# A decoder layer with four mixers on one core: one product with ones in place of four in the Conformer norm, and other places and loads for the MLP's forms and last weights

## The chip, the core and the metric

The kernel runs on one core of one Trainium2 chip. The core has five engines, which work side by side and each take their instructions in order: TensorE (PE) multiplies matrices into PSUM, VectorE (DVE), ScalarE (ACT) and GpSimd (POOL) work elementwise, and SyncE (SP) issues DMA transfers. POOL and ACT issue transfers too. PE appears in two rows of the profile: PE for the products, PEld for the weight loads, which run beside them. SBUF is the memory that the engines work in, DRAM the large one behind it.

The metric is device microseconds (us) of one launch, as the median of the runs. Besides, one execution was taken by the hardware profiler; every row of the trace comes from that one.

## The reference, cut to what matters

One layer of a decoder is computed for 1024 prompt tokens and 8 x 8 sample tokens, 1088 in all, with D = 1024 and everything in float32:

```python
h = rmsnorm(x, norm_mix_g) * (1 + sc1) + sh1
# four mixers, each 512 wide, from one input projection of h:
# HGRN2, RWKV-7, Conformer convolution, RG-LRU
u = cf[..., :W] * sigmoid(cf[..., W:])
yc = causal_dwconv(s_cf, u, cf_dw, cf_dw_b)
mu = mean(yc); var = mean(square(yc - mu))           # over the 512 channels
y_cf = silu((yc - mu) * rsqrt(var + 1e-5) * cf_ln_g + cf_ln_b)
out = sum_b(sigmoid(h @ w_gate + b_gate)_b * (y_b @ w_branch_b)) @ w_out
x = x + g1 * out
h2 = rmsnorm(x, norm_mlp_g) * (1 + sc2) + sh2
x = x + g2 * (square(relu(h2 @ w_mlp1)) @ w_mlp2)    # 1024 -> 4096 -> 1024
y = rmsnorm(x, norm_final_g)
```

The states of the mixers are outputs as well. The scales, shifts and factors sc, sh and g come from a small projection of a conditioning vector, one for the prompt and one for each of the eight samples.

## The kernel before, in words

**Layout.** Channels lie on the partitions and tokens along the free axis, so a tile is 128 channels by up to 1088 tokens. The tokens are cut in three ways: in CHUNKS of 364, 362 and 362, in two halves (columns) of 544, and in four quarters of 272 (QU).

**Products.** A float32 product is made of three products in the faster fp32r type: both factors are split into a rounded high part and the low rest, and hi x hi, lo x hi and hi x lo are added up in PSUM. `split` (L308) does it: ACT writes the high part, DVE subtracts it for the low part. `weights` (L151) does this for a block of four 128 x 128 weights: SP loads it into `wst` (3 buffers), and the split goes to `whi` and `wlo` (4 buffers). Products with `ones`, a 128 x 128 matrix of ones, sum over the partitions; they are in plain float32, which the trace records as two passes for each.

**The order of the work.** The program is laid out when it is built: a scheduler with a model of each engine's time decides the order of the instructions on every engine, by their dependencies and by priorities (`high_priority(offset=PRIO)` draws weights and evacuations ahead). Tiles of one tag rotate through a fixed number of buffers, and a pool that is closed gives its space to the pools opened after it. So where a tile lies decides what it must wait for.

**Stages.** 1. The first norm. 2. The mixers: the string ROUNDS lists, in four rounds, the steps of RWKV (r), HGRN2 (h), the Conformer (c), the RG-LRU (l), the Conformer norm (n, in the last round only), the conditioning (a) and the 32 gate products (g), which depend on nothing but h and fill PE while the recurrences run. 3. The merge of the branches, in the order RG-LRU, RWKV, Conformer, HGRN2. 4. The output projection with `w_out`, one half of the tokens after the other; POOL's queue writes the new x to DRAM (`xsp`). 5. MLP1. 6. MLP2 with the last norm.

**The Conformer norm**, `cf_norm` (L971). The four channel tiles X[0] to X[3] of 128 channels come back from DRAM. For each of the three chunks, four products with ones (L980-981) add the tiles up into `cm`, DVE subtracts the mean from each (L983), ACT squares each and four more products with ones (L988) give `cvar`. Ln and Exp make the inverse root, and the scaled tiles go back to DRAM for the merge.

**MLP1** (L1340-1388) uses seven products of blocks where a 2 x 2 block product has eight (Strassen's scheme in Winograd's form). `column_forms(c)` (L1284) normalises the half c of x and makes the seven forms B11, B21, T1 to T4 and B22 of it, each of them four tiles of 272 columns, split in high and low. The pools `resb` and `resa` hold x's two halves on the right of SBUF; the forms and `xw` (further weight forms) stand on the left, in the place of the output projection's pools. `seven_weights` (L212) loads four blocks of W1, makes seven forms of them and splits each; the first four forms made go to the pool `wp`, the others to `xw`. `seven` (L263) issues the seven products of one of 16 pairs of hidden blocks, and `evac` squares the positive part, splits it and writes it to DRAM (`asc`) by POOL's queue. Column 1's forms are made after the output projection, with twice the usual priority, and the first weights are asked for after them.

**MLP2** (L1391-1463) sums over 32 hidden blocks in six GROUPS. The first two blocks are kept in SBUF (`KK`). The others are loaded by SP's queue into tiles `ah` and `al` of 1088 columns, NA = 9 buffers of each; a block's high and its low tile have 544 KB each. `gemm_quarters` (L186) makes the products of one group for one of eight output tiles, and `ev` adds the result to R[mt]; in the second group (gi = 1) the saved x is loaded as `xr`, in one buffer, and added as well. The last group goes through the tokens in three columns of work: quarters (0, 1), quarter 2, quarter 3, each over eight output tiles, and builds its weights anew for each. Behind each column stands its norm (L1448-1462): one product with ones for each quarter, Ln, Exp, and the scaling of eight tiles, by ACT and POOL for columns 1 and 2 and for tiles 2 and 5 of column 3, else by DVE.

Of the kernel before, what the change touches and what calls it, by code (L numbers as in the profile page):

```python
# [31 lines left out]
GN_EPS = 64e-5  # L32
LN_EPS = 1e-5
# [57 lines left out]
class Net:  # L91
# [59 lines left out]
    def weights(self, ap, prio=True):  # L151

        with self.tc.high_priority(offset=PRIO) if prio else nullcontext():
            st = self.wp.tile([128, 4, 128], F32, name="wst", tag="wst", bufs=WST)
            hi = self.wp.tile([128, 4, 128], F32R, name="whi", tag="whi", bufs=WHI)
            lo = self.wp.tile([128, 4, 128], F32R, name="wlo", tag="wlo", bufs=WHI)
# [29 lines left out]
    def gemm_quarters(self, parts, X, evac, groups):  # L186
# [4 lines left out]
        for j, (ap, ks) in enumerate(parts):  # L191
            hi, lo = self.weights(ap)
# [57 lines left out]
    def product(self, ps, W, X, cs, start=True):  # L250

        hi, lo = W
        xh, xl = X
        for c in cs:
            for i in range(4):
                self.mm(ps[:, c, :QU], hi[:, i, :], xh[c][i], start=start and i == 0, stop=False)
                self.mm(ps[:, c, :QU], lo[:, i, :], xh[c][i], start=False, stop=False)
                self.mm(ps[:, c, :QU], hi[:, i, :], xl[c][i], start=False, stop=i == 3)
# [712 lines left out]
    def cf_norm(self):  # L971
# [121 lines left out]
PRIO = 3000  # L1093
WST, WHI = 3, 4
# [7 lines left out]
def trunk_kernel(ctx: ExitStack, tc: tile.TileContext, A):  # L1102
# [147 lines left out]
    pools = right(last, "resb"), right(ractx, "resa")  # L1250
# [18 lines left out]
    def add_sq(acc, r, mt, pool):  # L1269
        t = pool.tile([128, HALF], F32, name="sqt", tag="sqt", bufs=2)[:, :r.shape[-1]] if mt else None  # L1270
        net.sumsq(acc, r, t)
# [12 lines left out]
    def column_forms(c):  # L1284
# [9 lines left out]
        def split_form(f, i, src):  # L1294
            net.split(F[f][0][c][i], F[f][1][c][i], src)

# [7 lines left out]
        part = lambda k, h: R[:, k, h * QU:h * QU + QU]  # L1304
        for f, o in (("B11", 0), ("B21", 4)):
            for i in range(4):
                normed(i + o)
                split_form(f, i, part(i + o, 0))

        for f, out, a, b in (("T1", (0, 0), (0, 1), (0, 0)), ("T2", (0, 0), (4, 1), (0, 0)),  # L1310
                             ("T3", (0, 1), (4, 1), (0, 1)), ("T4", (4, 0), (4, 0), (0, 0))):
            for i in range(4):
                net.tt(part(i + out[0], out[1]), part(i + a[0], a[1]), part(i + b[0], b[1]), OP.subtract)
                split_form(f, i, part(i + out[0], out[1]))
        for i in range(4):
            split_form("B22", i, part(i + 4, 1))

    with ExitStack() as m:
# [8 lines left out]
        for half in range(2):  # L1327
            R, accs, rstd = RR[half]
            for mt in range(8):
                def ev(ps, n0, n):  # L1330
                    r = R[:, mt, n0:n0 + n]
                    add_resid(r, half * HALF + n0, ps[:, :n], n, mt, 2)
                    add_sq(accs[:, n0:n0 + n], r, mt, ops[half])
# [7 lines left out]
    for c in range(2):  # L1341
        fpool = left(fctx, f"forms{c}")
        for f in F:
            for p in range(2):
                F[f][p][c] = [fpool.tile([128, QU], F32R, name=f"{f}{'hl'[p]}{c}{i}") for i in range(4)]
    net.xw = left(fctx, "xw")
    column_forms(0)
    net.stage.close()
    with tc.tile_pool(name="pq", bufs=4, space=PSUM, reuse_waits="tile") as net.pq:
# [8 lines left out]
        with ExitStack() as m:  # L1358
# [17 lines left out]
            for j in range(16):  # L1376
                W = net.seven_weights((A["w1"][2 * j], A["w1"][2 * j + 1]))
# [10 lines left out]
        fctx.close()  # L1388


        with ExitStack() as m:  # L1391
            rp, ap_ = left(m, "resid"), left(m, "ap")
# [3 lines left out]
            GROUPS = ((0, 1), (2, 3, 4, 5, 6, 7), tuple(range(8, 16)), tuple(range(16, 24)), (24, 25, 26, 27), (28, 29, 30, 31))  # L1396
# [16 lines left out]
            for gi, ks in enumerate(GROUPS):  # L1413
                final = gi == len(GROUPS) - 1
                Xs = {}
                for k in ks:
                    if gi == 0:
                        Xs[k] = Kept(2 * k), Kept(4 + 2 * k)
                    else:
                        t = [ap_.tile([128, NT], F32R, name=f"a{p}", tag=f"a{p}", bufs=NA) for p in "hl"]  # L1420
                        for x, d in zip(t, asc):
                            nc.sync.dma_start(x.bitcast(F32), d[k].bitcast(F32))
# [3 lines left out]
                def ev(ps, qs):  # L1426
# [6 lines left out]
                    if final:  # L1433
                        sl = slice(qs[0] * QU, qs[-1] * QU + QU)
                        add_sq(accs[:, sl], r[:, sl], mt, ap_)

                for cs in (((0, 1),), ((2,),), ((3,),)) if final else (((0, 1), (2, 3)),):
                    for mt in range(8):
# [117 lines left out]
```

## Time and profile before

| | us |
|---|---|
| runs (3) | 2477.72, 2475.24, 2478.2 |
| their median | 2477.72 |
| the profiled execution | 2474.55 |
| its span, first to last instruction | 2472.8 |
| DVE, ACT and POOL busy | 1375.8, 1035.5, 306.0 |

The profile's span is 1.75 us shorter than the same execution's time. Busy times are those of instructions that compute; issuing a transfer, waiting and branching are not counted. A row of a timeline names the line of the code and the operation, then output<-input by the names of the tiles, the shape of the input or output, and xN, where N instructions of one kind are taken together. Where a helper records an operation, all its uses have the helper's line (L98 for ACT, L101 and L104 for DVE, L107 for PE), and the names of the tiles tell them apart. The granted clock is the share of full speed that PE was allowed.

### The profile page before, as it was taken

What the parts mean: (1) busy time and instruction counts of PE and PEld (TensorE: products, weight loads), DVE (VectorE), ACT (ScalarE), POOL (GpSimd) and SP (SyncE); (2) the same over time, 40 slices, a digit from 0 to 9 for tenths busy, and PEclk for the clock granted to TensorE, in tenths of its full rate; (3) what the DMA queues carried; (4) which work ended last, traced back from release to release, by engine and by line L of the source; (5) the groups of instructions that cost most, each with busy time, mean ns of one, the idle gap of its engine ahead of it and who ended that gap; (6) DMA issues with size and microseconds to landing.
All of it is one profiled execution on the core that took longest, in us unless ns stands there. A gap on an engine that the chain in (4) does not pass through costs nothing.

```text
span 2472.8 us, 46690 instructions
## 1 busy us (share of the span) xinstructions
PE 2394.4 (97%) x19150; PEld 2236.7 (90%) x19150; DVE 1375.8 (56%) x2540; ACT 1035.5 (42%) x1849; POOL 306.0 (12%) x479
## 2 busy tenths in 40 slices
PE   6999999999999999999999999997999999999996
PEld 4998898988998988889888999997999998999996
DVE  6666445746266473656734676768655552422247
ACT  5522545225344234542256553455666663111115
POOL 0102200012101021000111000001222221000003
PEclk9999999999999999999999999999999999999998
DMA  7333221241322232213322464532655657425244
GB/s 258 129 88 95 94 70 63 80 111 57 106 69 70 81 94 91 74 64 85 100 90 107 148 215 164 175 120 89 184 155 154 158 151 266 156 100 189 68 153 135
DMA packets 189140, 300.45 MB, mean 122 GB/s; under 512 B 57320, under 2 KB 105400, under 8 KB 188928
## 3 DMA queue, kind: packets, MB, share of 16 engines
q1 hardware_dynamic: 138512, 217.79, 27.9%
q0 software_dynamic: 47104, 74.44, 9.9%
q10 hardware_dynamic: 3312, 5.25, 0.6%
q8 instruction: 150, 2.46, 0.4%
q14 instruction: 62, 0.51, 0.1%
HBM read 211.29 MB, written 81.66 MB: 118 GB/s over the span
## 4 chain that ended last, share of the span: by engine, by line
PE 83%; DVE 7%; DMA 4%; ACT 3%; issue 2%; SPq 0%; ACTq 0%; DVEq 0%; POOL 0%; POOLq 0%
PE pg L107 57%; PE pa L107 6%; PE pe L107 4%; PE sm L107 2%; PE pc L107 2%; PE pb L107 2%; PE pu L107 2%; DVE X L101 2%; PE ada L107 1%; PE G L107 1%; PE pyr L107 1%; PE po L107 1%; DMA adaw<-ada 1%; DVE wlo L101 1%; DMA g<-gst 1%
## 5 line engine op out<-in xcount | busy, mean ns | idle before, releaser
L107 PE MATMUL pg<-Hh,whi 128*128 128x362 f32 (+1 forms) x1872 | 625.9, 335 | 1.0 <-ACT gst L98 0.7
L107 PE MATMUL pg<-Hh,wlo 128*128 128x362 f32 (+1 forms) x1872 | 626.6, 335 | 0.0
L107 PE MATMUL pg<-Hl,whi 128*128 128x362 f32 (+1 forms) x1872 | 621.0, 334 | 0.0
L98 ACT ACTIVATE whi<-wst 128x512 fp32r<-128x512 f32 (+1 forms) x404 | 250.0, 620 | 609.7 <-PE pg L107 534.8
L101 DVE TENSOR_TENSOR wlo<-wst,whi 128x512 fp32r<-128x512 f32 (+1 forms) x404 | 278.5, 690 | 380.9 <-ACT whi L98 380.1
L107 PEld LDWEIGHTS pg<-Hh,whi 128*128 128x128 f32 x1872 | 352.6, 188 | 12.5 <-issue 2.3
L107 PEld LDWEIGHTS pg<-Hl,whi 128*128 128x128 f32 x1872 | 352.3, 189 | 8.5 <-DVE Hl L104 0.8
L107 PEld LDWEIGHTS pg<-Hh,wlo 128*128 128x128 f32 x1872 | 352.9, 189 | 7.6
L107 PE MATMUL pg<-ah,whi 128*128 128x272 f32 x960 | 276.4, 290 | 2.9 <-ACT whi L98 2.9
L107 PE MATMUL pg<-ah,wlo 128*128 128x272 f32 x960 | 277.3, 290 | 1.4 <-DVE wlo L101 1.4
L107 PE MATMUL pg<-al,whi 128*128 128x272 f32 x960 | 273.8, 290 | 0.0
L107 PEld LDWEIGHTS pg<-ah,whi 128*128 128x128 f32 x960 | 181.9, 190 | 3.5 <-ACT whi L98 3.3
L107 PEld LDWEIGHTS pg<-ah,wlo 128*128 128x128 f32 x960 | 182.1, 190 | 2.2 <-DVE wlo L101 2.0
L107 PEld LDWEIGHTS pg<-al,whi 128*128 128x128 f32 x960 | 180.3, 190 | 0.0
L104 DVE SCALAR_TENSOR_TENSOR cacc<-u,pv,cacc 128x1024 f32<-128x1024 f32 x120 | 153.8, 1281 | 2.1
L104 DVE SCALAR_TENSOR_TENSOR R<-pg,mod,R 128x544 f32<-128x544 f32 (+2 forms) x120 | 65.7, 570 | 136.7 <-PE pg L107 136.7
L107 PE MATMUL pg<-yh,whi 128*128 128x362 f32 (+1 forms) x384 | 127.5, 332 | 1.1 <-DVE gt L101 1.1
L107 PE MATMUL pg<-yh,wlo 128*128 128x362 f32 (+1 forms) x384 | 126.6, 330 | 0.0
L107 PE MATMUL pg<-yl,whi 128*128 128x362 f32 (+1 forms) x384 | 126.2, 329 | 0.0
L1181 POOL DMA_DIRECT2D g<-gst x96 | 53.5, 557 | 390.0 <-ACT gst L98 377.5
L98 ACT ACTIVATE gst<-pg 128x362 f32<-128x362 f32 (+1 forms) x96 | 45.4, 473 | 126.2 <-PE pg L107 111.6
L699 POOL TENSOR_SCALAR sp<-St,dec 128x64 f32<-128x64 f32 x60 | 58.5, 975 | 229.2 <-DVE St L104 208.0
(443 smaller groups left out, 4757.3 us busy)
## 6 DMA issues: line engine op xcount, KB each, us to landing
wst<-w SPq DMA_DIRECT2D x136, 256.0 KB, 3.3
adaw<-ada SPq DMA_DIRECT2D x48, 512.0 KB, 7.2
wst<-w_in SPq DMA_DIRECT2D x92, 256.0 KB, 2.9
gt<-g SPq DMA_DIRECT2D x32, 544.0 KB, 4.1
wst<-w_gate SPq DMA_DIRECT2D x64, 256.0 KB, 2.9
ah<-ah POOLq DMA_DIRECT2D x60, 272.0 KB, 2.7
al<-al POOLq DMA_DIRECT2D x60, 272.0 KB, 4.3
ah<-ah SPq DMA_DIRECT2D x30, 544.0 KB, 9.0
```

Source lines behind the costliest of these rows:

```text
L98: return self.nc.scalar.activation(out, in_, func, bias=bias, scale=scale)
L101: return self.nc.vector.tensor_tensor(out, a, b, op=op)
L104: return self.nc.vector.scalar_tensor_tensor(out, a, s, b, op0=op0, op1=op1)
L107: return self.nc.tensor.matmul(out, lhsT, rhs, start=start, stop=stop, skip_group_check=True)
L699: nc.gpsimd.tensor_scalar(sp, St, dec[:, c:c + 1], None, op0=OP.mult)
L1181: nc.gpsimd.dma_start(d[:, n0:n0 + n], t[:, :n])
```

## The change

**The Conformer norm.** The four tiles of a chunk are added on DVE into `acc`, a slice of the tile that the inverse root uses later, and one product with ones is made of it. The squares are summed into the same slice by `sumsq` (L395: ACT squares, DVE adds), and again one product is made.

```diff
+            acc = rs_[:, n0:n0 + n]
+            self.tt(acc, X[0][:, n0:n0 + n], X[1][:, n0:n0 + n], OP.add)
+            for j in (2, 3):
+                self.tt(acc, acc, X[j][:, n0:n0 + n], OP.add)
             ps = self.pgt("cm")
-            for j in range(4):
-                self.mm(ps[:, :n], self.ones, X[j][:, n0:n0 + n], start=j == 0, stop=j == 3)
+            self.mm(ps[:, :n], self.ones, acc)
...
+            for j in range(4):
+                self.sumsq(acc, X[j][:, n0:n0 + n], self.lp.tile([128, 364], F32, name="gst", bufs=2)[:, :n] if j else None)
             ps = self.pgt("cvar")
-            for j in range(4):
-                s = self.lp.tile([128, 364], F32, name="gst", bufs=2)[:, :n]
-                self.act(s, X[j][:, n0:n0 + n], AF.Square)
-                self.mm(ps[:, :n], self.ones, s, start=j == 0, stop=j == 3)
+            self.mm(ps[:, :n], self.ones, acc)
```

**The weight forms' place and the column forms.** `xw` moves to the right side, between the pools of x's two halves. Which of the seven weight forms lie in `wp` and which in `xw` changes. The first pair's weights, W0, are asked for after column 0's forms, before column 1's. The four tiles of a form become one tile of four slices (and `product` picks a slice); column 0's steps take four slices at once, column 1's two.

```diff
-                pool = self.wp if next(n) < 4 else self.xw
+                pool = self.wp if next(n) in (0, 1, 5, 6) else self.xw
...
-    pools = right(last, "resb"), right(ractx, "resa")
+    xctx = ExitStack()
+    pools = [right(last, "resb")]
+    net.xw = right(xctx, "xw")
+    pools.append(right(ractx, "resa"))
...
+        step = 2 if c else 4
+        part = lambda k, h: R[:, k:k + step, h * QU:h * QU + QU]
+
+        def split_form(f, i, src):
+            net.split(F[f][0][c][:, i:i + step], F[f][1][c][:, i:i + step], src)
...
-                F[f][p][c] = [fpool.tile([128, QU], F32R, name=f"{f}{'hl'[p]}{c}{i}") for i in range(4)]
-    net.xw = left(fctx, "xw")
+                F[f][p][c] = fpool.tile([128, 4, QU], F32R, name=f"{f}{'hl'[p]}{c}")
     column_forms(0)
+    W0 = net.seven_weights((A["w1"][0], A["w1"][1]))
     net.stage.close()
...
-                W = net.seven_weights((A["w1"][2 * j], A["w1"][2 * j + 1]))
+                W = net.seven_weights((A["w1"][2 * j], A["w1"][2 * j + 1])) if j else W0
```

**MLP2's loads.** The first loaded group has two blocks in place of six, the big groups follow, and POOL's queue issues the loads. The pools are opened in another order, so that the `ah` and `al` tiles come to lie lowest, and `xr` and the last norm's squares move to a pool of their own.

```diff
-            rp, ap_ = left(m, "resid"), left(m, "ap")
+            ap_, rp, mp = left(m, "ap"), left(m, "resid"), left(m, "misc")
...
-            GROUPS = ((0, 1), (2, 3, 4, 5, 6, 7), tuple(range(8, 16)), tuple(range(16, 24)), (24, 25, 26, 27), (28, 29, 30, 31))
+            GROUPS = ((0, 1), (2, 3)) + tuple(tuple(range(i, i + 8)) for i in (4, 12, 20)) + ((28, 29, 30, 31),)
...
-                            nc.sync.dma_start(x.bitcast(F32), d[k].bitcast(F32))
+                            nc.gpsimd.dma_start(x.bitcast(F32), d[k].bitcast(F32))
```

**The last group's weights and norm.** The eight blocks of the last group's weights are built once, in the first column, into a pool `fw` with eight buffers, which takes the place of `resb`, and are used again in the other columns. The norm of a column becomes a function `last_norm`, issued after the third output tile of the next column. DVE does the scaling in one instruction, except for tiles 2 and 5 of column 3.

```diff
+                if final:
+                    last.close()
+                    fw, kept = right(m, "fw"), []
+                for n, qs in enumerate(columns):
+                    for mt in range(8):
...
+                            if n == 0:
+                                kept.append(net.weights(A["w2"][ks[0] // 4, mt], pool=fw, bufs=8))
+                            net.gemm_quarters([(kept[mt], ks)], Y, ev, (qs,))
...
+                        if final and n and mt == 2:
+                            last_norm(columns[n - 1])
+                if final:
+                    last_norm(columns[-1])
...
                     for k in range(KB8):
                         r, t = R[k][:, sl], rstd[:, sl]
-                        if cs[0] != (3,) or k % 3 == 2:
+                        if qs == (3,) and k % 3 == 2:
                             net.act(r, r, AF.Copy, scale=net.p("norm_final_g", k))
                             nc.gpsimd.tensor_tensor(r, r, t, op=OP.mult)
                         else:
                             net.stt(r, r, net.p("norm_final_g", k), t, OP.mult, OP.mult)
```

More of the change, by code (lines that the diff above doesn't have):

```diff
@@ L32 @@
 GN_EPS = 64e-5
+PRIO = 3000
+WST, WHI = 3, 4
 LN_EPS = 1e-5
@@ L148, in pgt, with weights @@
         return self.pg.tile([128, 512], F32, name=name, tag="pg")
-    def weights(self, ap, prio=True):
+    def weights(self, ap, prio=True, pool=None, bufs=WHI):
         with self.tc.high_priority(offset=PRIO) if prio else nullcontext():
             st = self.wp.tile([128, 4, 128], F32, name="wst", tag="wst", bufs=WST)
-            hi = self.wp.tile([128, 4, 128], F32R, name="whi", tag="whi", bufs=WHI)
-            lo = self.wp.tile([128, 4, 128], F32R, name="wlo", tag="wlo", bufs=WHI)
+            hi = (pool or self.wp).tile([128, 4, 128], F32R, name="whi", tag="whi", bufs=bufs)
+            lo = (pool or self.wp).tile([128, 4, 128], F32R, name="wlo", tag="wlo", bufs=bufs)
             n = ap.shape[1]
@@ L190, in gemm_quarters @@
         xh, xl = X
-        for j, (ap, ks) in enumerate(parts):
-            hi, lo = self.weights(ap)
+        for j, (W, ks) in enumerate(parts):
+            hi, lo = W if isinstance(W, tuple) else self.weights(W)
             for g, qs in enumerate(groups):
@@ L1090, in lru_block @@
         nc.gpsimd.dma_start(self.ysc[3][j], hs[:, :NT])
-PRIO = 3000
-WST, WHI = 3, 4
 NG = 5
@@ L1267, in add_resid, with add_sq @@
                 net.tt(r[:, e:n], r[:, e:n], t.rearrange("p s t -> p (s t)"), OP.add)
-    def add_sq(acc, r, mt, pool):
-        t = pool.tile([128, HALF], F32, name="sqt", tag="sqt", bufs=2)[:, :r.shape[-1]] if mt else None
+    def add_sq(acc, r, mt, pool, width):
+        t = pool.tile([128, width], F32, name="sqt", tag="sqt", bufs=2)[:, :r.shape[-1]] if mt else None
         net.sumsq(acc, r, t)
@@ L1434, in ev, with last_norm @@
                         sl = slice(qs[0] * QU, qs[-1] * QU + QU)
[L1435 to L1454 removed]
+                        add_sq(accs[:, sl], r[:, sl], mt, mp, HALF)
+                def last_norm(qs):
+                    sl = slice(qs[0] * QU, qs[-1] * QU + QU)
+                    ps = net.pqt("rms")
+                    for i, q in enumerate(qs):
+                        s = slice(q * QU, q * QU + QU)
+                        net.mm(ps[:, i, :QU], net.ones, accs[:, s])
+                        net.lnp(rstd[:, s], ps[:, i, :QU], 1.0 / D, net.eps)
+                        net.exph(rstd[:, s])
                     for k in range(KB8):
                         r, t = R[k][:, sl], rstd[:, sl]
[L1457 removed]
+                        if qs == (3,) and k % 3 == 2:
                             net.act(r, r, AF.Copy, scale=net.p("norm_final_g", k))
@@ L1462, in trunk_kernel @@
                         (nc.sync if k % 2 else nc.scalar).dma_start(A["y"][k][:, sl], r)
-    last.close()
+                columns = ((0, 1), (2,), (3,)) if final else (((0, 1), (2, 3)),)
+                if final:
[3 more added lines that the diff above has]
+                    for mt in range(8):
+                        if not final:
+                            net.gemm_quarters(parts(ks, mt), Y, ev, qs)
+                        else:
+                            if n == 0:
+                                kept.append(net.weights(A["w2"][ks[0] // 4, mt], pool=fw, bufs=8))
+                            net.gemm_quarters([(kept[mt], ks)], Y, ev, (qs,))
+                        if gi == 1:
+                            x = mp.tile([128, NT], F32, name="xr", tag="xr", bufs=1)
+                            for h in range(2):
+                                nc.sync.dma_start(x[:, h * HALF:h * HALF + HALF], xsp[h][:, mt, :])
+                            net.tt(R[mt], R[mt], x, OP.add)
+                        if final and n and mt == 2:
+                            last_norm(columns[n - 1])
+                if final:
+                    last_norm(columns[-1])
 def _pack(i):
```

35 lines of the change are left out of this document (10 added, 25 removed).

## The prediction

> **What bounds the kernel now.** I read the page first, then PE's waits, then a table of busy time by stage, and only then single rows. The page's head, and PE's busy tenths in 40 slices of 61.8 us:
>
> ```profile
> span 2472.8 us, 46690 instructions
> ...
> PE 2394.4 (97%) x19150; PEld 2236.7 (90%) x19150; DVE 1375.8 (56%) x2540; ACT 1035.5 (42%) x1849; POOL 306.0 (12%) x479
> ...
> PE   6999999999999999999999999997999999999996
> ```
>
> TensorE (PE) is busy for 97% of the span. Only three of its slices fall below 9: the first, which the change does not touch, the one near 1700 us, and the last. So time is to be had in two ways: take products away where PE never rests, or fill those holes. The longest entries of PE's waits that the change can touch (total us, times, longest):
>
> ```profile
> PE rms L107 <- DVE accs L101: 13.0, 3, 8.2
> ...
> PE pe L107 <- DVE x L101: 2.8, 1, 2.8
> PE pe L107 <- ACT whi L98: 2.5, 1, 2.5
> PE pe L107 <- DVE wlo L101: 2.5, 1, 2.5
> ```
>
> Busy time by stage, from the windows view: window, its length, then busy us (and instructions) of PE, weight loads, DVE, ACT, POOL, then the granted clock, DMA share and GB/s:
>
> ```profile
> 1296.00:1330.00 34.00, 33.51 (x213) 24.12 (x214) 8.94 (x20) 14.96 (x30) 3.33 (x7) 1.00 0.07 25
> 1350.00:1386.00 36.00, 34.63 (x615) 32.81 (x614) 35.41 (x54) 25.92 (x34) 2.85 (x5) 1.00 0.44 149
> 1690.00:1740.00 50.00, 37.18 (x238) 34.02 (x237) 43.08 (x97) 34.21 (x84) 7.97 (x15) 0.90 0.33 93
> 1699.00:1733.00 34.00, 22.45 (x127) 20.28 (x128) 33.74 (x78) 25.07 (x65) 3.58 (x7) 0.85 0.24 66
> 1750.00:2050.00 300.00, 300.00 (x2383) 300.00 (x2382) 171.38 (x262) 179.42 (x308) 76.75 (x112) 1.00 0.59 155
> 2060.00:2100.00 40.00, 34.37 (x252) 33.12 (x251) 9.73 (x24) 13.30 (x29) 1.35 (x2) 0.96 0.93 330
> 2100.00:2420.00 320.00, 320.00 (x2551) 320.00 (x2550) 112.31 (x232) 44.93 (x71) 0.00 (x0) 1.00 0.38 133
> 2420.00:2462.00 42.00, 31.19 (x223) 30.17 (x221) 33.28 (x60) 24.20 (x48) 19.66 (x16) 0.88 0.49 153
> ```
>
> The two long MLP rows give PE's pace when nothing holds it: 300/2383 = 0.126 us a product of 272 columns. Against that pace I count what each disturbed window loses, idle time and slowed clock together. MLP1's start: 238 x 0.126 = 30.0 us of 50, so 20 lost. MLP1 to MLP2: 252 x 0.126 = 31.8 of 40, so 8 lost. The last window: 223 x 0.126 = 28.1 of 42, of which I give 1 back for the slower f32 products of the norm, so 13 lost. The four parts of the change sit on these three windows and on the Conformer norm.
>
> **Part A, the Conformer norm.** PE's timeline there (start, length, instruction; a product in f32 counts as two passes):
>
> ```profile
> 1297.12 2.61 PE L107 MATMUL cm<-cx,ones 128*128 128x364 f32 x8
> 1299.65 0.34 PE L107 MATMUL pst<-vk 128*64 128x64 f32 x4
> ...
> 1307.52 1.49 PE L107 MATMUL cvar<-gst,ones 128*128 128x364 f32 x4
> 1308.94 0.44 PE L107 MATMUL pu<-p,G 64*64 64x64 f32 x4
> ```
>
> Eight passes take 1299.65 - 1297.12 = 2.53 us, 0.63 a product; four of the variance 1.42, 0.71 a product. Each chunk keeps one of four, so nine of each go: 9 x 0.63 + 9 x 0.71 = 12.1 us of PE. PE was busy 33.51 of those 34 us, and what fills it (the gate products) is left, so all of it could count. In exchange DVE gets three adds of tiles and three of squares a chunk, 18 in all, priced by an add of the same shape:
>
> ```profile
> L101 DVE TENSOR_TENSOR M<-M,gt 128x362 f32<-128x362 f32 x48 | 25.6, 536 | 1.4
> ```
>
> 18 x 0.536 = 9.6 us, on an engine busy 8.94 of 34: they lie beside PE's other work. ACT's squares stay 12. What waits behind an add is RWKV's state update on DVE, and PE's chain behind that; the norm's result itself is wanted only by the third branch of the merge. If that cover is gone, the adds cost at most their 9.6 us. The accumulator is now written at the first add instead of at Ln; its buffer comes from the rotation after those of the four tiles and was released earlier than the last of them, so I cost that at nothing. Against the full 12.1 speaks 1350 to 1386: HGRN2's last block keeps DVE busy 35.41 of 36 there, and PE bridges it with the same gate products, which now come due sooner. Bounds 0 and -12.1, a stall included; I take -9.5, nearer to the full price since PE itself was busy 34.63 of that window.
>
> **Part B, MLP1's start.** From 1699 to 1733 DVE is busy 33.74 of 34: it is the bound, and PE waits for it. Rows of DVE:
>
> ```profile
> 1694.77 0.44 DVE L101 TENSOR_TENSOR accs<-accs,sqt 128x272 f32<-128x272 f32 x1 [0.56 <-ACT sqt L98]
> 1695.12 0.69 DVE L101 TENSOR_TENSOR wcm<-wst 128x512 f32<-128x512 f32 x1
> ...
> 1700.61 5.12 DVE L104 SCALAR_TENSOR_TENSOR rh<-rh,mod,rstd 128x480 f32<-128x480 f32 x8
> 1705.65 0.68 DVE L101 TENSOR_TENSOR wlo<-wst,whi 128x512 fp32r<-128x512 f32 x1
> ...
> 1708.41 1.49 DVE L101 TENSOR_TENSOR B11l<-rh,B11h 128x272 fp32r<-128x272 f32 x4
> ```
>
> The first tile of the pool xw is written right after the last read of the old stage's sqt, which lay in its place; and one form of the weights that PE waits for (wlo, 2.5 us in the waits) stands behind eight normalisations. The change puts xw where nothing of that stage lies and issues the first weights before column 1's forms. About five of the 0.68 us steps then leave the DVE-bound stretch, starts being 0.60 apart: 3.0 us. They land before 1695, beside the output projection. Column 1 makes 28 low parts and 16 sums. Four in 1.49 us are 0.35 each, 15.4; done in pairs they are 22 of 544 columns:
>
> ```profile
> L101 DVE TENSOR_TENSOR al<-x,ah 128x544 fp32r<-128x544 f32 x60 | 42.1, 721 | 8.6 <-ACT ah L98 8.1 <-DMA al<-al 0.5
> ```
>
> which is 15.9 by the duration and 14.0 if starts overlap by the 0.09 us seen above: 1.4 saved, or nothing. So DVE's stretch shrinks by 3.0 to 4.4. On top come PE's two waits on weights (2.5 each) and part of the clock, granted at 0.90 over 50 us. Column 0 in whole fours makes its steps coarser beside the output projection, whose evacuations queue behind them; that may cost a microsecond or two. Bounds -2 and -14; I take -7. What is late next is DVE again, with column 1's last forms.
>
> **Part C, from MLP1 to MLP2.** The chain of waits there, and the usual landing time of the weights from the table of DMA issues:
>
> ```profile
> 2059.19 15.34 DMA ah<-ah
> ...
> 2074.59 9.61 DMA wst<-w
> ```
>
> ```profile
> wst<-w SPq DMA_DIRECT2D x136, 256.0 KB, 3.3
> ```
>
> A block of weights that lands in 3.3 us took 9.61, and PE lost 8 us in that window, because six hidden blocks (12 tiles of 544 KB) and the weights went through SP's queue together. The change asks for two blocks (4 tiles) in the first loaded group, 24 us of products ahead of the big one, and gives the tiles to POOL's queue. By the code each new tile lies exactly on one forms tile, and the first of these are released early in MLP1's last pair. But two things are added. The residual xr must now come within 3.0 us an output tile (24 products) instead of 9, in one buffer; its adds slip, with a group's time of slack. And MLP1's last writes now share a queue with the loads:
>
> ```profile
> ACT ah L98 <- DMA ah<-ah: 4.9, 1, 4.9
> ```
>
> Behind that 4.9 us wait on ACT stand the evacuations of MLP2's first products. With up to 18 tiles ahead it may triple, and PE has two output tiles, 6 us, of cover. Bounds -8 and +9; I take -5.
>
> The Trainium skill, page "DMA: Bandwidth & Descriptors", section "Issuing engines are not separate DMA queues", speaks against the move: DMAs of sync, scalar and gpsimd run on the same 16 engines, and another issuer saves only issue time. By it the queue is worth nothing, and only the regrouping is left; the rival "same engines" below is what that would do.
>
> **Part D, the end of MLP2.** DVE, POOL, then PE's last product:
>
> ```profile
> 2433.32 1.58 DVE L101 TENSOR_TENSOR accs<-accs,sqt 128x272 f32<-128x272 f32 x1
> ...
> 2446.55 0.43 DVE L101 TENSOR_TENSOR accs<-accs,sqt 128x272 f32<-128x272 f32 x1
> ```
>
> ```profile
> 2431.48 12.88 POOL L1459 TENSOR_TENSOR R<-R,rstd 128x544 f32<-128x544 f32 x8 [361.59 <-ACT rstd L98]
> ```
>
> ```profile
> 2461.55 0.28 PE L107 MATMUL pg<-al,whi 128*128 128x272 f32 x1
> ```
>
> While POOL multiplies, an add that takes 0.43 takes 1.58, and the norm's product waits up to 8.2 us for such adds with PE's queue standing behind it. The change takes 16 of the 18 POOL multiplications away, builds the eight last weights once (16 builds and loads fewer) and issues each column's norm after three tiles of the next. So of the 13 lost nearly all can return. Against it, DVE gets the multiplications:
>
> ```profile
> L104 DVE SCALAR_TENSOR_TENSOR R<-R,pv,rstd x6: 489/490/1099, 2465.9 to 2469.1; 128x272 f32<-128x272 f32 x6
> ```
>
> 8 x 0.49 = 3.9 us in the last column, whose 96 products last 12.1; I let DVE end 2 us further behind PE. From the last product to the end (2472.8 - 2461.8 = 11 us) the steps stay. Bounds -13 and -6; I take -11.
>
> **Sum.** -9.5 - 7 - 5 - 11 = -32.5 us. The profiled execution took 2474.55 (span 2472.8 and 1.75 around it), 3.2 under the median of the runs, 2477.72. From the profile 2474.55 - 32.5 = 2442.1; on the median's scale 2477.72 - 32.5 = 2445.2. MLP1's and MLP2's steady parts stay at 0.126 us a product. The smallest change that measurement can tell from none is taken as 0.2%, 5 us.
>
> **Rivals.** *Same engines*: the weights are still late after MLP1, since the bytes are the same; C gives 0, and the time is 2450. For it speaks 330 GB/s and 0.93 DMA share in that window; against it, that the bytes before the second group fall from 12 tiles to 4.
>
> *The filler runs out*: the order of all engines is planned at build time, and the gate products saved up by A are gone before HGRN2's last block is done; DVE's 35.41 of 36 speaks for it. A gives 0, and if the planner also leaves the first weights behind column 1's normalisations, B gives 2: 2445.2 + 9.5 + 5 = 2460.
>
> *Slower: loads one at a time on POOL's queue.* MLP2's groups of eight have nine buffers, so at each of the three boundaries six tiles must come within about 7 us (48 products and one block's own). A boundary loses 6t - 7 for t us a tile; from t = 3.0 on, three boundaries eat the whole gain. The nearest row of a tile of that size on POOL's queue:
>
> ```profile
> y<-cx POOLq DMA_DIRECT2D x4, 544.0 KB, 4.9
> ```
>
> Lone and unoverlapped, t = 4.9 loses 22.4 at each, 67 in all: 2512. Against it: a POOL issue need not wait for the one before to land, and the 320.00 of 320 holds such a boundary crossed on SP's queue without loss.
>
> **How the numbers follow.** The forecast has 0.70, *same engines* 0.11, *the filler runs out* 0.08: faster by over 0.2% 0.89. Loads one at a time, whole or in part, 0.07 for slower; 0.04 for gains that return as waits and leave less than 5 us. The range takes the first three: all four parts near their good bounds give 2477.7 - 47 = 2431, and C's loss or the run-out filler gives up to 2464. I say 2429 to 2464, which leaves out the slower case, the same case and tails of the parts.
>
> **What would show it.** A: six products of ones instead of 24, and 1350 to 1386 as full on PE as now. B: the waits on whi and wlo near 1700 gone, DVE still full but some 5 us shorter. C: a granted clock of 1.00 from 2060 on, weights landing in about 3 us. D: no PE wait on accs but the very last, adds at 0.43 throughout, the last product some 30 us earlier. The prediction is wrong if PE shows idle time at MLP2's group boundaries, or new waits between 1340 and 1400 that add up to A's gain.

## The result and the profile after

The changed kernel takes 2461.70 us (median of 5 runs, 2458.66 to 2467.12) against 2477.72 us before (5 runs, 2473.48 to 2479.85). The ratio is 0.9939, with a 95% interval of 0.9927 to 0.9951. So 16.0 us are gained, where 32.5 were forecast, just under half; the time lies at the upper end of the stated range. The profiled execution has a span of 2459.9 us. In the changed kernel's rows the helpers' lines are two higher than before (L109 for PE, L100 for ACT, L103 and L106 for DVE).

The head of the page after:

```profile
span 2459.9 us, 46415 instructions
...
PE 2387.9 (97%) x19114; PEld 2235.8 (91%) x19114; DVE 1368.8 (56%) x2503; ACT 1016.7 (41%) x1788; POOL 319.1 (13%) x523
...
PE   6999999999999999999997999998899999999997
```

The last slice is a little fuller than before, the holes at MLP1's start are still there, and there is a new one: a 7 in the 22nd slice, at about 1320 us. The waits of PE that name it, and the others that are left (total us, times, longest):

```profile
PE pg L109 <- ACT gst L100: 8.1, 1, 8.1
...
PE pa L109 <- ACT T2h L100: 3.6, 1, 3.6
...
PE pc L109 <- ACT T4h L100: 2.4, 1, 2.4
```

The first is new: PE waits once for 8.1 us until ACT has copied a gate product out of PSUM; before, such waits came to 0.7 us in all. Busy time by stage after, columns as in the prediction:

```profile
1296.00:1330.00 34.00, 29.51 (x210) 21.68 (x205) 18.64 (x40) 18.64 (x36) 4.93 (x9) 0.90 0.23 83
...
1350.00:1386.00 36.00, 36.00 (x621) 34.66 (x621) 29.32 (x49) 19.18 (x27) 5.52 (x12) 0.98 0.34 108
...
2060.00:2100.00 40.00, 40.00 (x322) 40.00 (x321) 18.74 (x50) 16.77 (x36) 12.88 (x23) 1.00 0.94 335
2100.00:2420.00 320.00, 319.62 (x2540) 318.96 (x2539) 104.76 (x209) 39.83 (x63) 22.04 (x42) 1.00 0.38 132
2420.00:2446.00 26.00, 24.41 (x187) 23.52 (x185) 21.57 (x53) 8.07 (x21) 0.00 (x0) 1.00 0.37 130
```

The window from MLP1 to MLP2 is full now (40.00 of 40, clock 1.00), and the end of MLP2 nearly so (24.41 of 26). The window of the Conformer norm, which was full before (33.51 of 34), is not: 29.51, at a clock of 0.90.

**One product, two times.** Both programs have the same instructions in the same order on every engine up to the Conformer norm. Yet this product of RWKV, the same one in both, started here before and after:

```profile
1286.38 0.44 PE L107 MATMUL pu<-p,G 64*64 64x64 f32 x4
```

```profile
1291.65 0.44 PE L109 MATMUL pu<-p,G 64*64 64x64 f32 x4
```

The same work took 5.27 us longer in the profiled execution after. So absolute times of the two traces must not be compared; stages are measured from one event of a trace to another. From the tile views (first and last start of PE's products by kind), in us:

| stage | before | after |
|---|---|---|
| to RWKV's last `pu` | 1325.6 | 1317.2 |
| from there to the merge's first product | 55.2 | 75.6 |
| the merge, first to last product | 208.5 | 204.0 |
| from there to MLP1's last B11 product | 441.9 | 437.2 |
| MLP2's first product to its first loaded one | 33.1 | 30.0 |
| from there to PE's last hidden product | 381.7 | 366.0 |
| from there to the end of the span | 11.3 | 14.4 |

RWKV ends earlier (13.7 us, with the 5.27 taken out), and all of it and more is lost before the merge. MLP2 gains 18.8, and the tail gives back 3.1.

### The profile page after: what moved, and what is told of

It reads as the page before. It is cut to its first block, busy times and chain, and to the rows that moved or that the text cites. A ratio compares the mean times of both kernels' runs of the same rounds, so it can differ in the third digit from the quotient of the medians.

```text
span 2459.9 us, 46415 instructions
## 1 busy us (share of the span) xinstructions
PE 2387.9 (97%) x19114; PEld 2235.8 (91%) x19114; DVE 1368.8 (56%) x2503; ACT 1016.7 (41%) x1788; POOL 319.1 (13%) x523
## 3 DMA queue, kind: packets, MB, share of 16 engines
q0 software_dynamic: 55744, 107.87, 13.4%
## 4 chain that ended last, share of the span: by engine, by line
PE 77%; issue 10%; DVE 7%; DMA 4%; ACT 3%; POOL 1%; ACTq 0%; DVEq 0%; POOLq 0%
PE pg L109 50%; PE pa L109 5%; PE pe L109 3%; PE sm L109 3%; PE pc L109 2%; PE pb L109 2%; PE pu L109 2%; DVE X L103 2%; PE ada L109 2%; DMA al<-al 1%; PE G L109 1%; PE pyr L109 1%; PE po L109 1%; DMA ah<-ah 1%; DMA adaw<-ada 1%
## 5 line engine op out<-in xcount | busy, mean ns | idle before, releaser
L109 PE MATMUL pg<-Hh,whi 128*128 128x362 f32 (+1 forms) x1872 | 629.2, 337 | 8.1 <-ACT gst L100 8.1
L109 PE MATMUL pg<-Hh,wlo 128*128 128x362 f32 (+1 forms) x1872 | 629.5, 336 | 0.0
L109 PE MATMUL pg<-Hl,whi 128*128 128x362 f32 (+1 forms) x1872 | 622.8, 335 | 0.0
L103 DVE TENSOR_TENSOR wlo<-wst,whi 128x512 fp32r<-128x512 f32 (+1 forms) x388 | 262.1, 677 | 428.4 <-ACT whi L100 427.0
L100 ACT ACTIVATE whi<-wst 128x512 fp32r<-128x512 f32 (+1 forms) x388 | 239.6, 619 | 604.3 <-PE pg L109 495.7
L109 PEld LDWEIGHTS pg<-Hh,whi 128*128 128x128 f32 x1872 | 355.3, 190 | 19.3 <-ACT gst L100 8.4
L109 PEld LDWEIGHTS pg<-Hh,wlo 128*128 128x128 f32 x1872 | 355.6, 190 | 7.7 <-issue 0.3
L109 PEld LDWEIGHTS pg<-Hl,whi 128*128 128x128 f32 x1872 | 354.3, 190 | 8.5 <-issue 1.2
L109 PE MATMUL pg<-ah,whi 128*128 128x272 f32 x960 | 275.0, 289 | 0.4 <-DVE R L106 0.4
L109 PE MATMUL pg<-ah,wlo 128*128 128x272 f32 x960 | 274.7, 288 | 0.0
L109 PE MATMUL pg<-al,whi 128*128 128x272 f32 x960 | 270.7, 289 | 0.3 <-DMA al<-al 0.2
L109 PEld LDWEIGHTS pg<-ah,whi 128*128 128x128 f32 x960 | 180.4, 188 | 0.9 <-DVE R L106 0.6
L109 PEld LDWEIGHTS pg<-ah,wlo 128*128 128x128 f32 x960 | 180.7, 188 | 0.1
L109 PEld LDWEIGHTS pg<-al,whi 128*128 128x128 f32 x960 | 178.0, 188 | 0.8 <-DMA al<-al 0.8
L106 DVE SCALAR_TENSOR_TENSOR cacc<-u,pv,cacc 128x1024 f32<-128x1024 f32 x120 | 153.7, 1281 | 2.1
L109 PE MATMUL pg<-yh,whi 128*128 128x362 f32 (+1 forms) x384 | 126.5, 329 | 0.0
L109 PE MATMUL pg<-yh,wlo 128*128 128x362 f32 (+1 forms) x384 | 126.4, 329 | 0.0
L109 PE MATMUL pg<-yl,whi 128*128 128x362 f32 (+1 forms) x384 | 125.7, 328 | 0.0
L106 DVE SCALAR_TENSOR_TENSOR R<-pg,mod,R 128x544 f32<-128x544 f32 (+2 forms) x120 | 65.5, 569 | 100.5 <-PE pg L109 100.4
L100 ACT ACTIVATE gst<-pg 128x362 f32<-128x362 f32 (+1 forms) x96 | 45.3, 473 | 127.1 <-PE pg L109 113.9
```

Source lines behind the costliest of these rows:

```text
L100: return self.nc.scalar.activation(out, in_, func, bias=bias, scale=scale)
L103: return self.nc.vector.tensor_tensor(out, a, b, op=op)
L106: return self.nc.vector.scalar_tensor_tensor(out, a, s, b, op0=op0, op1=op1)
L109: return self.nc.tensor.matmul(out, lhsT, rhs, start=start, stop=stop, skip_group_check=True)
```

## The experiments

Each kernel ran in five rounds beside the kernel before. Parts A to D are those of the prediction: the Conformer norm, MLP1's start, MLP2's loads, the last group.

| kernel | median, us | ratio to before | 95% interval |
|---|---|---|---|
| before with A alone | 2479.20 | 1.0008 | 0.9999 to 1.0018 |
| before with B alone | 2467.21 | 0.9960 | 0.9944 to 0.9976 |
| before with C alone | 2477.15 | 0.9997 | 0.9987 to 1.0007 |
| before with D alone | 2466.35 | 0.9955 | 0.9939 to 0.9971 |
| after without A | 2456.44 | 0.9909 | 0.9894 to 0.9924 |
| after without C | 2456.92 | 0.9916 | 0.9904 to 0.9929 |
| after, Silu late | 2451.20 | 0.9889 | 0.9875 to 0.9902 |
| after, loads on SP | 2466.82 | 0.9949 | 0.9935 to 0.9963 |
| after, stores on POOL | 2459.31 | 0.9923 | 0.9911 to 0.9936 |
| after, Silu late and stores on POOL | 2452.74 | 0.9900 | 0.9886 to 0.9915 |
| after, Silu late, other PSUM tiles | 2491.50 | 1.0057 | 1.0045 to 1.0070 |
| after, Silu late, without C | 2450.77 | 0.9885 | 0.9868 to 0.9901 |

**The four parts, each alone.** The edits are the parts of the diff above, each put on the kernel before: `cf_norm` for A; `xw`, W0 and the steps of the forms for B; GROUPS, the loads' queue and the order of the pools for C; `fw`, `kept` and `last_norm` for D.

> The kernel before with part A alone (the Conformer norm). Two theories. ORDER: the trace of the changed kernel runs the same instructions as before up to about 1290 us, and from there to the end of the merge it loses 2.3 us more than before, because the plan now alternates the Conformer's Silu with RWKV's Ln and Exp and HGRN2's sigmoids on ACT (six more table loads at 1.28 us) and PE waits 8.1 us for a gate evacuation behind them. Then A alone gives 0 to +4 us: 2478 to 2482, with the same six extra table loads and the same wait of about 8 us. FORECAST: A gives -9.5 and it is another part that failed: 2468.

Measured: 2479.20, against 2477.55 beside it. The trace has the wait of 8.0 us for a gate evacuation and the same order on ACT as the changed kernel.

> The kernel before with part B alone (place of the weight forms, first weights ahead of column 1's forms, forms in fours and pairs). FORECAST: -7, 2471. TRACE ACCOUNT of the changed kernel: from the end of the merge to MLP1's steady part it gains 4.8 us, 3.3 of them already in the output projection: 2473. If B gives 0 or less than 2, its gain in the changed kernel comes from something that another part moved.

Measured: 2467.21, a gain of 10.3, more than either number. By the stages, 5.2 come ahead of MLP1's end, where B was expected to work (the stage from the merge to MLP1's last B11 product has 436.7 in place of 441.9), and 7.2 behind MLP1 (below); the merge took 2.3 more in this execution.

> The kernel before with part C alone (two blocks in the first loaded group, loads on POOL's queue, pools in another order). FORECAST: -5, 2473. TRACE ACCOUNT: the 8 us lost between MLP1 and MLP2 are gone in the changed kernel (40 of 40 us busy): -8, 2470.

Measured: 2477.15. By its stages MLP2 gains 6.0 and the tail loses 1.7, which would be -4.3; the interval of the ratio reaches from -3.2 to +1.7. Neither the forecast nor the trace account is borne out. C closes the hole, but the time does not show it; 1.6 of the tail's 1.7 lie behind the last output store (last section), and where the rest went stays open.

> The kernel before with part D alone (last weights kept, a column's norm behind three tiles of the next, scaling on DVE). FORECAST: -11, 2467. TRACE ACCOUNT: of the 13 us lost in the last window about 2.5 are left, and the tail from PE's last product to the end is 14.1 us long in place of 11: -13 + 2.5 + 3.1 = -7.4, 2470. If the four parts alone add up to about -16, they add; if they add up to -30, they take from one another when together.

Measured: 2466.35, a gain of 11.2, as forecast.

The four alone add up to +1.7 - 10.3 - 0.4 - 11.2 = -20.2, the change together to -16.0. So two terms of the prediction failed: A gains nothing, and C gains nothing that shows. The experiments that follow go after these two.

**The changed kernel without A.** The edit gives `cf_norm` its old text.

> The changed kernel with the old Conformer norm (parts B, C and D without A). A alone measured +2. If A costs the same inside the changed kernel, this one takes 2457 to 2460 and its ACT has six table loads fewer. FORECAST (A gives -9.5): 2471. Single parts measured -10.3, -0.4 and -11.2, which would add up to 2455.6; if B and C earn some of the same time between MLP1 and MLP2, as the stages of the single-part traces say (30.1 us from the first kept product to the first loaded one with B alone, with C alone and with all, 33.1 before), it is some 3 to 5 more.

Measured: 2456.44. Without A the change is 5.3 us faster than with it (2461.70). The cost looks larger than alone (1.7), but the intervals are too wide to be sure of that.

**Why A costs.** What ACT did from 1328 us on in the changed kernel (timeline: start, length, operation):

```profile
1328.64 1.17 ACT L100 ACTIVATE rs<-sm,epst 128x364 f32<-128x364 f32 x2 [1.32 <-PE sm L109]
1329.83 1.28 ACT L100 ACT_TABLE_LOAD   x1
1331.12 1.30 ACT L100 ACTIVATE cx<-cx,pv 128x1088 f32<-128x1088 f32 x1
1332.44 1.28 ACT L100 ACT_TABLE_LOAD   x1
1333.74 0.56 ACT L100 ACTIVATE rs<-sm,epst 128x362 f32<-128x362 f32 x1
...
1344.07 2.48 ACT L100 ACTIVATE cx<-cx,pv 128x1088 f32<-128x1088 f32 x2
...
1346.97 0.45 ACT L100 ACTIVATE gst<-pg 128x364 f32<-128x364 f32 x1
```

The `cx` rows are the Conformer's Silu, `rs` is the inverse root of RWKV's last norm. They need different function tables, and each change of table is a load of 1.28 us. The counts from 1290 to 1400 us, first before, then after:

```profile
L315 ACT ACT_TABLE_LOAD x3 | 3.8, 1283 | 0.1
L98 ACT ACT_TABLE_LOAD x3 | 3.8, 1283 | 0.1
```

```profile
L100 ACT ACT_TABLE_LOAD x8 | 10.3, 1283 | 0.1
...
L317 ACT ACT_TABLE_LOAD x3 | 3.8, 1283 | 0.1
```

Six loads became eleven. Behind them stands the copy `gst<-pg` at 1346.97, for which PE waits:

```profile
1339.09 0.32 PE L109 MATMUL pg<-Hl,whi 128*128 128x362 f32 x1
1347.48 0.67 PE L109 MATMUL pg<-Hh,whi 128*128 128x364 f32 x1 [8.06 <-ACT gst L100]
1347.94 0.51 PE L109 MATMUL pg<-Hh,wlo 128*128 128x364 f32 x1
1348.25 0.50 PE L109 MATMUL pg<-Hl,whi 128*128 128x364 f32 x1
```

After the wait the products start 0.30 us apart; at full clock such products start 0.16 to 0.17 apart (399 to 407 us, for one). The hole costs twice.

The Trainium skill has the rule for the first part (page "ScalarE: Activation LUTs", section "Table sets: the hidden batching unit"): calls of one table set are to be done together. Its example puts a load at about 2.7 us; in this trace a load takes 1.283 us, and the next operation starts 0.02 us behind it. The experiment batches the calls so: the four Silu are made to come behind the last Exp of HGRN2's scores.

```diff
-            self.act(x, x, AF.Silu, ...)
+            self.after(self.act(x, x, AF.Silu, ...), self.hg_exp)
...
-            self.act(X[:, :N], X[:, :N], AF.Exp)
+            self.hg_exp = self.act(X[:, :N], X[:, :N], AF.Exp)
```

> The changed kernel with one more dependency: the four Silu of the Conformer norm come behind the last Exp of HGRN2's score blocks on ACT, so that they no longer stand between RWKV's Ln and Exp and HGRN2's sigmoids. The plan has 50 table loads as before the change, in place of 56. ORDER theory: the wait of 8.1 us for a gate evacuation goes, and with it the windows of half clock behind it; 2461.7 - 8 to -12 = 2450 to 2454. RIVAL (PE has too few gate products left, and the hole only moves): PE idles as long at another place before the merge, 2460 to 2464. A part of the RIVAL would be the hole from 1304 to 1323 us, which this edit does not touch.

Measured: 2451.20, 10.5 less than the changed kernel and 5.2 less than without A. The wait of 8.1 us is gone from the list, the program has six table loads fewer. With this order A gains, but not 12.1. So the order on ACT cost 10.5, and that much of A's failure is shown.

**Where the rest of A's 12.1 us went.** Busy time of the kernel before, then of the changed kernel, then with the late Silu, over the same stretch:

```profile
1304.00:1323.00 19.00, 19.00 (x112) 12.87 (x111) 4.39 (x11) 7.74 (x15) 1.33 (x3) 1.00 0.00 1
1323.00:1350.00 27.00, 27.00 (x159) 24.20 (x158) 10.44 (x12) 20.85 (x26) 4.37 (x8) 1.00 0.54 196
```

```profile
1304.00:1323.00 19.00, 14.69 (x113) 9.04 (x113) 12.39 (x29) 10.72 (x24) 2.81 (x5) 0.84 0.23 77
1323.00:1350.00 27.00, 18.94 (x94) 17.00 (x93) 10.25 (x10) 25.18 (x25) 3.35 (x6) 0.88 0.29 109
```

```profile
1304.00:1323.00 19.00, 15.36 (x95) 10.41 (x96) 9.22 (x21) 10.35 (x19) 2.35 (x4) 0.82 0.27 98
1323.00:1350.00 27.00, 26.82 (x314) 24.61 (x314) 24.29 (x31) 19.78 (x25) 3.17 (x5) 1.00 0.17 63
1350.00:1386.00 36.00, 35.24 (x461) 33.88 (x462) 21.75 (x34) 23.45 (x32) 6.09 (x13) 1.00 0.54 187
```

After, 46 - 33.63 = 12.4 us are idle, and the lower clock takes about 14.69 x 0.16 + 18.94 x 0.12 = 4.6 more: 17.0 against 12.1 saved, a loss of 4.9 (without A measured: 5.3). With the late Silu 3.6 + 0.2 + 0.8 = 4.6 are idle and the clock takes 15.36 x 0.18 = 2.8: 7.4 against 12.1, a gain of 4.7 (measured: 5.2). This is an estimate, since the windows stand at fixed times of three executions that are some us apart, and since the kernel before was itself idle for 1.4 us from 1350 to 1386. The account holds to about 1 us in both.

What is left is the stretch from 1304 to 1323, in which RWKV makes its last steps. The same view of the kernel before, of the products in the gates' PSUM tiles alone (`pg`), 1300 to 1316:

```profile
1300.00:1316.00 16.00, 0.00 (x0) 0.00 (x0) 0.00 (x0) 0.00 (x0) 1.00 0.06 18
```

There was no gate product in it. What filled PE between RWKV's steps were the norm's own products of ones, the very ones that the change thins out: `cm` and `cvar` took 5.19 + 6.28 = 11.5 of PE's 15.5 busy us there. By the code, the norm's sums and the gate products share three PSUM tiles in turn, so that the gate products behind the norm can't start until its sums are read. An experiment gave the norm's sums the tiles of RWKV's small products.

```diff
-            ps = self.pgt("cm")
+            ps = self.pmt("cm")
...
-            ps = self.pgt("cvar")
+            ps = self.pmt("cvar")
```

> The changed kernel with the Silu mended, and with the norm's six products of ones in the PSUM tiles of RWKV's small products in place of those of the gate products. BANKS theory: between 1304 and 1323 us PE finds no gate products because the norm's sums take the three PSUM tiles in which these are added up; with other tiles the plan puts gate products between RWKV's last steps and the norm behind HGRN2's scores. Then PE is full while RWKV ends, but the gate products are gone when HGRN2's scores come, which before the change needed them: 2449 to 2455, with the holes in the stretch of HGRN2's scores. RIVAL (gate products suffice for both): the hole goes without return, 2446.

Measured: 2491.50, 40 us slower than the late Silu alone; far outside what either theory expected. The plan moved the norm behind HGRN2's scores and put gate products between RWKV's steps (10.2 us of them from 1300 to 1316). Then PE stood idle half of the time:

```profile
1323.00:1339.00 16.00, 8.45 (x146) 5.40 (x148) 8.79 (x10) 12.11 (x13) 1.21 (x2) 0.61 0.04 17
1339.00:1350.00 11.00, 2.92 (x55) 2.82 (x44) 11.00 (x19) 5.98 (x6) 0.00 (x0) 0.50 0.13 51
1350.00:1386.00 36.00, 20.04 (x324) 15.01 (x323) 21.40 (x43) 15.41 (x26) 3.61 (x9) 0.59 0.08 31
```

PE is busy for 31 of 63 us, at 0.50 to 0.61 of the clock. It did not lack products: 216 in the gates' tiles (a gate and two projections of HGRN2) still ran from 1378 to 1417. They were held up. PE's last such product ahead of the hole, the first behind it, and ACT just before:

```profile
1312.86 0.32 PE L109 MATMUL pg<-Hl,whi 128*128 128x362 f32 x1
1378.35 0.67 PE L109 MATMUL pg<-Hh,whi 128*128 128x364 f32 x1 [3.54 <-ACT gst L100]
```

```profile
1377.18 0.51 ACT L100 ACTIVATE gst<-cx 128x362 f32<-128x362 f32 x1 [0.32 <-DVE crs L103]
1377.82 0.47 ACT L100 ACTIVATE gst<-pg 128x364 f32<-128x364 f32 x1
```

A gate's sums, ready by 1313, were copied out from 1377.82 on, right behind the norm's last square. By the code, the norm's squares and the gates' copies share the two buffers `gst`, the norm's come first, and the gate's three sums fill all three PSUM tiles. So when the norm moved back, the gates stood behind it. The run therefore decides neither theory: it does not show that gate products run out, and that the shared PSUM tiles alone keep them out of 1304 to 1323 stays argued.

**Why C gains nothing.** SP's timeline of the kernel before, and of B alone, ahead of MLP2 (SPq is the issuing of transfers on SP):

```profile
2024.40 30.22 SPq L159 DMA_DIRECT2D wst<-w  x8
2054.72 0.37 SPq L1422 DMA_DIRECT2D ah<-ah  x1
...
2064.04 0.33 SPq L159 DMA_DIRECT2D wst<-w  x1
```

```profile
2023.03 42.27 SPq L159 DMA_DIRECT2D wst<-w  x10
2065.41 0.39 SPq L1430 DMA_DIRECT2D ah<-ah  x1
...
2067.97 0.33 SPq L159 DMA_DIRECT2D wst<-w  x1
```

Before, ten big tiles stood in the queue ahead of the next weights. With B alone ten blocks of weights go first, the first tile is asked for 10.7 us later, and a block of weights follows four tiles, not ten. So B takes the hole away by itself: from MLP2's first product to PE's last it has 407.6 us against 414.8. By the code, the tiles now wait for other space, since `xw` no longer lies under them; which of B's edits does it was not tried. Two experiments show what of C is left.

```diff
-                            nc.gpsimd.dma_start(x.bitcast(F32), d[k].bitcast(F32))
+                            nc.sync.dma_start(x.bitcast(F32), d[k].bitcast(F32))
```

> The changed kernel with MLP2's loads back on SP's queue; the groups and the order of the pools stay. SAME ENGINES (another issuer is worth nothing, the regrouping did it): 2461 to 2463 and no PE idle time from 2060 to 2120. QUEUE (the weights' 256 KB must not stand behind the tiles of 544 KB in one queue): PE waits for whi or wlo again behind the first loaded group, +4 to +8: 2466 to 2470.

Measured: 2466.82, 5.1 more than the changed kernel. The intervals of the two ratios overlap (0.9935 to 0.9963 and 0.9927 to 0.9951), so the whole time does not settle it; the stage does. The wait is back (4.1 us for whi), and so are the hole and, in the chain of waits, a block of weights that takes 10.54 us:

```profile
2080.00:2100.00 20.00, 15.55 (x96) 14.43 (x95) 9.42 (x23) 4.09 (x10) 0.00 (x0) 0.83 0.88 326
```

```profile
2077.32 10.54 DMA wst<-w
```

From MLP2's first loaded product to PE's last it has 373.0 us; the six traces that have parts C and D with the loads on POOL's queue show 365.9 to 366.9. The tail gives 2.0 of these 7 back. The same bytes, the same groups: the queue made the difference. The rule of the Trainium skill weighed in the prediction (page "DMA: Bandwidth & Descriptors", section "Issuing engines are not separate DMA queues") would have given none; in this stage the measurement decides against it.

The second experiment leaves all of C out (old GROUPS, SP, old pools; A, B and D stay).

> The changed kernel without part C (old groups, loads on SP, old order of the pools; A, B and D stay). B alone already crossed from MLP1 to MLP2 without loss (30.1 us from the first kept product to the first loaded one, 33.1 before; 377.5 from there to the last, 381.7 before), while the new groups with the loads on SP lost 5.1. OVERLAP theory: with B, the old groups on SP lose nothing, C is worth 0 here: 2460 to 2463. FORECAST (C gives -5 whatever B does): 2467, with PE waits for whi between 2060 and 2100.

Measured: 2456.92, 4.8 less than with C, by medians measured at different times; the intervals of the two ratios, 0.9904 to 0.9929 and 0.9927 to 0.9951, just touch. PE is full from 2060 to 2420 without C too. In the stages that C touches, 2.8 us are saved without it: 1.3 in MLP2 and 1.5 in the tail. The new groups need POOL's queue; the old ones, with B, need neither.

**The tail.** In the changed kernel ACT's issuing of transfers (ACTq) stands at an output store while squares wait behind it:

```profile
2440.13 3.29 ACTq L1462 DMA_DIRECT2D y<-R  x4
2443.97 0.43 ACT L100 ACTIVATE sqt<-R 128x272 f32<-128x272 f32 x1 [4.03 <-DMA y<-R]
```

```diff
-                        (nc.sync if k % 2 else nc.scalar).dma_start(A["y"][k][:, sl], r)
+                        (nc.sync if k % 2 else nc.scalar if qs == (3,) else nc.gpsimd).dma_start(A["y"][k][:, sl], r)
```

> The changed kernel with the output stores of the first two columns issued by POOL where ACT issued them. In the changed kernel's trace ACT's queue stands for 3.3 us at such stores (each waits for DVE's scaling), the squares of the last tiles come 4.0 us late behind it, and PE's last product of ones waits 3.65 us. If that sets the tail (14.4 us from the last product to the end, 11.3 before), the tail shrinks by 2 to 3 us: 2459. RIVAL: DVE, which does the adds and the scaling one after the other, is late anyway: 2461 to 2462.

Measured: 2459.31, but the tail did not shrink: it has 15.2 us (14.4 after). The stores are gone from ACT, and the square still comes late, for DVE now:

```profile
2444.69 0.43 ACT L100 ACTIVATE sqt<-R 128x272 f32<-128x272 f32 x1 [4.02 <-DVE R L103]
```

The rival was right: DVE, with adds and scaling in turn, sets the tail. The 2.4 us lie within the scatter of the runs.

**Together.** Both mends in one kernel, and the late Silu without C:

> The changed kernel with both mends: the Silu behind HGRN2's Exp on ACT, and the output stores of columns 1 and 2 issued by POOL. Alone they measured 2451.2 and 2459.3 against 2461.7. They lie 1100 us apart, so they should add: 2448.8.

Measured: 2452.74. The stores add nothing.

> The changed kernel with the Silu mended and without part C: A (Silu behind HGRN2's Exp), B and D. The Silu mend measured -10.5 against the changed kernel, leaving C out -4.8. They touch different stretches, so ADDING: 2461.7 - 10.5 - 4.8 = 2446.4, the last product about 13 us from the end in place of 14.4. If C's cost of 4.8 was scatter in the stretch ahead of it (its own stages show only about 3: 1.4 in MLP2 and 1.5 in the tail), 2448 to 2451.

Measured: 2450.77; leaving C out adds nothing here that shows, though the same stages are again 2.9 us shorter (1.4 and 1.5). Its cost beside B is therefore not settled: between 0 and 5. The late Silu alone (2451.20) is about 10 us faster than the change and 26 faster than the kernel before; this last kernel is its equal with fewer edits.

## Why the prediction was right in parts only

**Part A, forecast -9.5, measured +1.7 alone and +5.3 inside the change.** The step that failed: "PE was busy 33.51 of those 34 us, and what fills it (the gate products) is left, so all of it could count." What filled most of it, from 1300 to 1316, was the norm itself (11.5 of 15.5 us). A full window says that PE has something to do, not that something else is waiting to be done. The second failing step: the norm's result "is wanted only by the third branch of the merge", so its steps were taken to stand in nobody's way. But ACT does them in a fixed order with HGRN2's sigmoids and the gate evacuations, and PE waited 8.1 us for one of these; with the Silu tied together 10.5 us came back. The adds on DVE, 18 at 0.53, were priced rightly, and PE waited no longer than 1.5 us at a time from 1300 to 1324, where they lie.

**Part B, forecast -7, measured -10.3 alone.** It gained more than forecast, and only in part where the prediction said. Ahead of MLP1's end it gave 5.2 (4.7 in the change), and 3.1 of these lie in the output projection, whose products spread over 98.4 us in place of 101.5: a wait of 2.8 us for DVE is gone there, where the prediction feared a loss. At MLP1's start the waits for whi and wlo are gone, as said, but others came in their place: 11.7 us before (T2l, x, whi, wlo), 11.6 with B alone (T2l, rms, T2h, B11l, T1l). The coarser steps of the forms may be why; it wasn't tried. The other 7.2 came from a place the prediction did not look at, SP's queue ahead of MLP2.

**Part C, forecast -5, measured -0.4 alone, and 0 to +5 beside B.** The hole was read rightly (8 us, weights behind big tiles in one queue), the remedy worked, and 40.00 of 40 us were full. The step that failed is the sum, which adds B and C as if they did not touch: B closes the same hole. A price was missing as well, about 2 us at the end of the span (last section). The rival *same engines* does not hold for the stage: on SP's queue it took 7 us more. *Loads one at a time* did not come: the boundaries were crossed with 319.62 of 320.

**Part D, forecast -11, measured -11.2.** With D alone the last hidden product comes 370.4 us after the first loaded one in place of 381.7, and the tail has 12.3 us, 1.0 more. In the changed kernel the tail is 3.1 longer, where 2 were allowed; 2.0 of these lie behind the last output store and come with C.

With A's and C's values inside the change, -32.5 becomes +5.3 - 10.3 + 0 - 11.2 = -16.2, against 16.0 measured; with C at the 2.8 us that its stages show it is -13.4, so the close fit is partly luck. The rival *the filler runs out* named 2460, near the 2461.70 measured, but not for its reason: products in the gates' tiles lasted until 1392 us, just ahead of the merge. No run here shows them running out.

## What to carry to other kernels

Before counting removed products as time, look at what PE would do in their place, row by row: a product between two steps of a recurrence may be filling for nothing. Buffers that two kinds of work share tie their order together: with other PSUM tiles, finished gate sums stood 65 us behind the squares that use the same two buffers. Where activation functions of different tables can be reordered by a planner, tie them together by hand, since each change costs 1.28 us and whatever waits behind it. Two remedies for one hole are worth one.

## What the runs showed of the hardware

The runs of one kernel differ by up to 11 us (the kernel before, beside the single parts: 2471.76 to 2482.81), and the granted clock mostly goes with it: the changed kernel took 2467.12 at a mean clock of 0.987 and 2458.66 at 0.990. In the trace the clock falls to half for one or more pieces of 3.41 us, as for 6.83 us around the end of the 8.06 us wait above. It can do so without a wait of PE, and in one execution and not in another: the stretch that both programs share has one such piece between 100 and 1290 us in the profile before and five after. One of the five began at 405.7 us, behind 16 products of only 8 columns; before, the same products left the clock alone:

```profile
400.66 1.95 PE L107 MATMUL po<-hq,sst 128*128 128x8 f32 x16
...
405.71 0.33 PE L107 MATMUL pg<-Hh,wlo 128*128 128x362 f32 x1
```

```profile
402.87 1.95 PE L109 MATMUL po<-hq,sst 128*128 128x8 f32 x16
...
406.13 0.51 PE L109 MATMUL pg<-Hh,wlo 128*128 128x364 f32 x1
```

The Trainium skill gives a reason (page "TensorE: Matmul & The Clock Gate", section "What's actually happening"): the clock is judged in windows of about 3.4 us that run free of the program. The trace agrees in the length of the pieces. So what a hole costs beyond its length differs from run to run.

The end of the span came later where POOL's queue had issued the tiles: SP's last store was issued at 2452.58 + 2.48 us in the changed kernel and the span ended 4.8 later; without C it was 2450.52 + 2.48 and 2.8 later. All traces agree: 4.4 to 5.5 in the seven where POOL issued MLP2's loads, 2.7 to 2.9 in the seven where SP did. Why, no run here tells.

```profile
2452.58 2.48 SPq L1462 DMA_DIRECT2D y<-R  x4
```

```profile
2450.52 2.48 SPq L1462 DMA_DIRECT2D y<-R  x4
```
